# One common rank for a background step's small TensorE products, 18 instructions behind the start of the step

## The chip, the cores and the metric

The kernel runs on 1 core of one Trainium2 chip. The metric is the device time of one execution in microseconds. Five engines work side by side: TensorE (PE, with its weight loads shown as PEld), VectorE (DVE), ScalarE (ACT), GpSimd (POOL) and SyncE (SP), which issues the transfers.

## The reference

One inference step of a two-layer decoder trunk in float32, for a prompt of 1024 rows and 8 samples of 8 rows, model width 1024. Layer 0's mixer joins gated linear attention (GLA) and a depthwise convolution of 31 taps; layer 1's joins dilated windowed attention (three patterns, 4 heads each, with cached keys and values for the samples) and a chunked gMLP. After each mixer comes a convolutional FFN of inner width 2816. Cut to what matters:

```
def trunk(x, gla_s, convb_buf, kv_bufs, ffn_buf, p):
    for layer in range(DEPTH):
        h = rmsnorm(x, p['norm_pre_mix'][layer])
        if layer % 2 == 0:
            y, s_new, cb_new = even_mixer(h, ...)      # GLA | Conformer conv
        else:
            y, kv_new, v_new = odd_mixer(h, ...)       # dilated attention | gMLP
        x = x + rmsnorm(y, p['norm_post_mix'][layer])
        h = rmsnorm(x, p['norm_pre_ffn'][layer])
        f, fb = conv_ffn(h, ffn_buf[layer], ...)       # (gelu(g) * val) @ w_down
        x = x + rmsnorm(f, p['norm_post_ffn'][layer])
```

The outputs are both groups' rows and all new states and caches.

## The kernel before, in words

The rows are cut in two halves: A holds prompt rows 0 to 511 (one piece of 512 columns), B holds rows 512 to 1023 and the 64 sample rows (two pieces of 288 columns). Activations lie transposed, features on partitions.

The large products, called main products here, go through `gemm` (L374): a weight column block of 1024 x 128 is fetched (raw), split into a high and a low part (whi on ACT or POOL, wlo on DVE or POOL), and for each of up to 8 blocks of the inner dimension three products are issued per piece (whi x hi, whi x lo, wlo x hi) into a PSUM tile "g". Their tiles in the profile are "g<-...".

Everything else of a mixer (GLA, convolution, attention, gMLP, norms, loads) is written as generators. `during` (L236) makes one the background of the following main products, and `gemm` calls `pump` (L242) after each inner block; `pump` runs as many steps of the generator (each up to its next `yield`) as the amount of main work since the last call is worth. `drain` (L253) runs what is left of a generator at once, outside `pump`. The steps' own products are small; they go through `tr` (L222, transposes) and `mm` (L226) into PSUM tiles "m", of which there are four, and are copied out by ACT, DVE or both. A float32 small product shows as two MATMUL records in the profile, a main product as one. `mm` is also called by `gemm`, and `tr` by main code such as `in_odd` (L1224).

The order of work on each engine is not written by hand. Each instruction is traced with a rank, the builder's running number `cur_priority`; each traced instruction raises the number by one. The builder then orders every engine's instructions in advance: in its own model of time, an engine takes the ready instruction of the lowest rank. `high_priority(offset)` sets the number to the current one less `offset` inside its block, and sets it back to the old value on leaving, so that instructions inside the block don't advance it. The weight fetches use it already: `chunk` (L355) gives them ranks 400 ahead (`self.ahead`, L359).

The stages, in the order of the trace, with their rough places in the span:

- 0 to 358: load, input projections of layer 0 for A and B; behind them convolution and GLA of A, then the norms of A.
- 358 to 840: FFN of A, layer 0. Behind it `mix0` (L1901): convolution (L838) and GLA (L918) of B, the copy of cache rows, and the FFN state's transposes. GLA's `pairs(lv)` (L951) issues per step four copies of the query (L959, two on ACT and two on POOL, first group of a level only), four small products, and two masked copies on DVE (L983).
- 840 to 1036: output projection of B, input projection of A for layer 1; behind it the norms of B and `sgu_prepare` (L1171), the transposes of the gMLP's masked weights.
- 1036 to 1600: FFN of B, layer 0; behind it `mix1(A)` (L1926): gMLP (L1322) and attention (L1372) of A. Then output projection and norms of A.
- 1600 to 1836: start of A's second FFN and, inside it, the input projection of B for layer 1; behind it the gMLP of B and the sample scores.
- 1836 to 2097: A's second FFN goes on; behind it the sample attention (L1700) and the attention of B. 2097 to 2192: the rest of that, drained, and the output projection of B.
- 2192 to 2738: rest of A's FFN, the norms of B, B's second FFN and the end.

The lines around the change:

```
    def pump(self, units):
        ...
        while self.acc > 0:
            w = next(self.bg, None)
            ...
            self.acc -= w
```

Of the kernel before, what the change touches and what calls it, by code (L numbers as in the profile page):

```python
# [2 lines left out]

# [1 line left out]

# [123 lines left out]
class Half:  # L129
    def __init__(self, idx):  # L130
        self.i = idx
        self.t0 = 512 * idx
        self.ns = NS if idx else 0
        self.n = 512 + self.ns
        self.pieces = [(0, 288), (288, 288)] if idx else [(0, 512)]
        self.blocks = [(b * P, P) for b in range(4)] + ([(512, NS)] if idx else [])


class Kern:
    def __init__(self, ctx, tc, I, O):  # L140
        self.tc, self.nc, self.I, self.O = tc, tc.nc, I, O
        self.uid = 0
        pool = lambda name, **kw: ctx.enter_context(tc.tile_pool(name=name, **kw))
        self.cp = pool("cp", bufs=1)
        self.dp = pool("dp", bufs=1, space=DRAM)
        self.ar = [pool("arA", bufs=24), pool("arB", bufs=24)]
        self.wp = pool("wp", bufs=3)
        self.ap = pool("ap", bufs=10)
        self.fp = pool("fp", bufs=2)
        self.np_ = pool("np", bufs=1)  # L150
        self.mp = pool("mp", bufs=2)
        self.pg = pool("pg", bufs=4, space=PSUM)
        self.pm = pool("pm", bufs=4, space=PSUM)
        self.halves = [Half(0), Half(1)]
        self.rr = 0
        self.copy_act = False
        self.urgent = [0, 0]
        self.bg = None
        self.ahead = 0

        self.nw, self.hi_act, self.lo_pool = 0, 0, 0


# [57 lines left out]

    def tr(self, out, in_):  # L222
        k = in_.shape[0]
        self.nc.tensor.transpose(out, in_, self.ident[:k, :k])  # L224

    def mm(self, out, l, r, start, stop):  # L226
        self.nc.tensor.matmul(out, l, r, start=start, stop=stop)  # L227

    def rstd(self, out, in_, scale):

# [11 lines left out]
    def pump(self, units):  # L242
        if self.bg is None:
            return
        self.acc += units * self.rate
        while self.acc > 0:
            w = next(self.bg, None)
            if w is None:
                self.bg = None
                return  # L250
            self.acc -= w
# [1761 lines left out]
```

## Time and profile before

| | us |
|---|---|
| median of 3 runs | 2743.64 |
| lowest and highest | 2735.56, 2754.35 |
| the profiled execution | 2739.51 |
| its span | 2737.7 |
| TensorE busy | 2602.5 |
| VectorE busy | 1750.0 |

The span is the time from the first to the last instruction of one profiled execution. Busy times are unions over an engine's instructions. A row of a timeline has the start, the length, the engine, the line, the operation, output<-inputs, the shape and the count; in brackets the engine's idle time before it and what ended it. A row of the waits has the time in all, how often, and the longest. PEclk is TensorE's granted clock as a share of full speed (2.4 GHz; the lower level is half of it).

### The profile page before, as it was taken

The page shows a single profiled execution, that of the slowest core. Times are in us where ns is not written, and L with a number is a line of the kernel's source. Part 1 is how long each engine was busy: PE and PEld are TensorE (multiplying, and loading weights), DVE is VectorE, ACT ScalarE, POOL GpSimd, SP SyncE. Part 2 cuts the span into 40 slices and gives each one's busy share as a digit, 9 for nine tenths or more (in the row PEclk, how much of TensorE's full clock was granted, in tenths as well). Part 3 has the DMA queues.
Part 4 walks back from the last instruction along what each step waited for, and adds up shares of the span by engine and source line. Part 5 has one row for each costly group of instructions (what it writes and reads, how often), then busy time and mean ns, then how long its engine had stood idle before and what let it go on. Part 6 is the DMA issues. An engine that isn't in the chain of part 4 may idle for free.

```text
span 2737.7 us, 43989 instructions
## 1 busy us (share of the span) xinstructions
PE 2602.5 (95%) x16517; PEld 2324.9 (85%) x16517; DVE 1750.0 (64%) x3045; ACT 963.7 (35%) x2022; POOL 1039.2 (38%) x1159
## 2 busy tenths in 40 slices
PE   7989999998999999999999999889999899999998
PEld 6779887786888779999999979877878678999998
DVE  4898369999577664655557784557665358555555
ACT  4343455433454222333323342113334343322223
POOL 2321333533235443242437533553213266333333
PEclk9999999999999999999999999999999799999999
DMA  7433354454544464332324335884454152422232
GB/s 218 127 99 92 91 194 148 151 161 146 173 126 134 144 192 121 115 96 81 89 70 137 122 112 177 234 247 136 124 169 133 34 172 85 141 78 74 82 91 82
DMA packets 505004, 355.83 MB, mean 130 GB/s; under 512 B 29547, under 2 KB 461282, under 8 KB 504015
## 3 DMA queue, kind: packets, MB, share of 16 engines
q1 hardware_dynamic: 504791, 353.01, 42.8%
q8 instruction: 131, 2.15, 0.3%
q14 instruction: 82, 0.67, 0.1%
HBM read 306.43 MB, written 75.97 MB: 140 GB/s over the span
## 4 chain that ended last, share of the span: by engine, by line
PE 62%; DVE 11%; DMA 6%; POOL 4%; issue 2%; ACT 2%; SPq 1%; POOLq 0%; DVEq 0%; ACTq 0%
PE g L227 55%; PE m L227 6%; DVE cv L200 3%; DMA kc<-qr 2%; PE m L224 2%; DVE wlo L371 2%; DVE c L200 1%; POOL whi L206 1%; DVE y L197 1%; SPq L188 1%; DVE y L200 1%; DMA raw<-in_w_down 1%; POOL ss L427 1%; DVE lo L197 1%; POOL w L1691 1%
## 5 line engine op out<-in xcount | busy, mean ns | idle before, releaser
L227 PE MATMUL g<-hi,whi 128*128 128x288 f32 (+2 forms) x4440 | 1272.6, 335 | 33.9 <-ACT hi L209 9.8
L227 PE MATMUL g<-lo,whi 128*128 128x288 f32 (+2 forms) x4440 | 1260.4, 332 | 5.3 <-DVE lo L197 5.3
L227 PE MATMUL g<-hi,wlo 128*128 128x288 f32 (+1 forms) x4416 | 1248.8, 332 | 4.2 <-DVE wlo L371 2.9
L227 PEld LDWEIGHTS g<-hi,whi 128*128 128x128 f32 (+1 forms) x4440 | 773.9, 191 | 108.3 <-issue 23.5
L227 PEld LDWEIGHTS g<-lo,whi 128*128 128x128 f32 (+1 forms) x4440 | 773.5, 190 | 68.0 <-DVE lo L197 7.7
L227 PEld LDWEIGHTS g<-hi,wlo 128*128 128x128 f32 x4416 | 768.6, 191 | 65.7 <-DVE wlo L371 4.1
L371 DVE TENSOR_TENSOR wlo<-raw,whi 128x1024 fp32r<-128x1024 f32 (+2 forms) x382 | 408.0, 1068 | 440.9 <-POOL whi L206 340.8
L206 POOL TENSOR_SCALAR whi<-raw 128x1024 fp32r<-128x1024 f32 (+2 forms) x307 | 318.3, 1037 | 704.2 <-PE g L227 568.2
L371 POOL TENSOR_TENSOR wlo<-raw,whi 128x1024 fp32r<-128x1024 f32 (+2 forms) x94 | 194.7, 2073 | 405.8 <-ACT whi L209 357.5
L200 DVE SCALAR_TENSOR_TENSOR c<-u,dw,c 128x512 f32<-128x512 f32 (+3 forms) x528 | 317.4, 638 | 44.5 <-ACT c L212 42.7
L209 ACT ACTIVATE whi<-raw 128x1024 fp32r<-128x1024 f32 (+3 forms) x171 | 145.0, 849 | 382.4 <-PE g L227 256.2
L209 ACT ACTIVATE u<-g 128x224 f32<-128x224 f32 (+2 forms) x352 | 129.1, 398 | 296.6 <-PE g L227 284.1
L200 DVE SCALAR_TENSOR_TENSOR cv<-u,cvw,cv 128x512 f32<-128x512 f32 (+21 forms) x240 | 192.6, 813 | 1.9
L197 DVE TENSOR_TENSOR y<-y,g 128x288 f32<-128x288 f32 (+3 forms) x240 | 120.2, 526 | 111.8 <-PE g L227 111.5
L212 ACT ACTIVATE c<-g,dw 128x288 f32<-128x288 f32 (+1 forms) x264 | 173.1, 657 | 2.0 <-DVE lo L197 1.0
L427 POOL TENSOR_TENSOR ss<-ss,sq 128x512 f32<-128x512 f32 (+1 forms) x75 | 121.3, 1618 | 40.8 <-ACT sq L212 37.7
L209 ACT ACTIVATE hi<-c 128x512 fp32r<-128x512 f32 (+1 forms) x88 | 57.9, 658 | 199.2 <-DVE c L197 199.1
L212 ACT ACTIVATE c<-c 128x512 f32<-128x512 f32 (+1 forms) x88 | 57.9, 658 | 145.0 <-DVE c L200 137.3
L600 POOL COPY last<-u 128x2 f32<-128x2 f32 x88 | 49.2, 559 | 115.1 <-ACT u L209 102.4
L212 ACT ACTIVATE sq<-y 128x512 f32<-128x512 f32 (+3 forms) x103 | 63.2, 622 | 83.9 <-POOL ss L427 44.3
L200 DVE SCALAR_TENSOR_TENSOR y<-y,vec,rb 128x512 f32<-128x512 f32 (+1 forms) x104 | 87.6, 909 | 7.0 <-ACT rb L209 7.0
L1691 POOL TENSOR_TENSOR w<-kc,kc 128x512 f32<-128x512 f32 x48 | 65.0, 1369 | 69.9 <-DMA kc<-qr 64.4
(288 smaller groups left out, 2246.0 us busy)
## 6 DMA issues: line engine op xcount, KB each, us to landing
raw<-in_w_up SPq DMA_DIRECT2D x176, 512.0 KB
raw<-in_w_down SPq DMA_DIRECT2D x128, 256.0 KB
raw<-in_w_in_odd SPq DMA_DIRECT2D x44, 512.0 KB
raw<-in_w_in_even SPq DMA_DIRECT2D x40, 512.0 KB
out_s_kv<-in_cache_c_w SPq DMA_DIRECT2D x32, 512.0 KB
raw<-in_w_down SPq DMA_DIRECT2D x64, 192.0 KB
xl<-x SPq DMA_DIRECT2D x40, 256.0 KB
kc<-in_cache_c_w SPq DMA_DIRECT2D x80, 128.0 KB
```

The source lines that it names most:

```text
L188: self.nc.sync.dma_start(out, in_)
L197: self.nc.vector.tensor_tensor(out=out, in0=a, in1=b, op=op)
L200: self.nc.vector.scalar_tensor_tensor(out=out, in0=a, scalar=s, in1=b, op0=op0, op1=op1)
L206: self.nc.gpsimd.tensor_scalar(out=out, in0=a, scalar1=s1, scalar2=s2, op0=op0, op1=op1)
L209: self.nc.scalar.activation(out, in_, AF.Copy, scale=scale)
L212: self.nc.scalar.activation(out, in_, func, **kw)
L224: self.nc.tensor.transpose(out, in_, self.ident[:k, :k])
L227: self.nc.tensor.matmul(out, l, r, start=start, stop=stop)
L371: eng.tensor_tensor(out=wlo[:, :nk, :m], in0=raw[:, :nk, :m], in1=whi[:, :nk, :m].bitcast(F32), op=ALU.subtract)
L427: eng.tensor_tensor(out=t, in0=t, in1=sq, op=ALU.add)
L600: self.nc.gpsimd.tensor_copy(self.last2[l][:, jt, :], u[:, 512:514])
L1691: nc.gpsimd.tensor_tensor(out=pr, in0=kc.rearrange("p i c -> p (i c)"), in1=q.rearrange("p i c -> p (i c)"), op=ALU.mult)
```

## The change

`pump` notes the rank at which a step starts (`place`). While a step runs, `tr` and `mm` trace their instruction inside `high_priority` with an offset that makes its rank `place + 18`, whatever its own place in the step. Instructions of the step on other engines and its transfers keep their ranks; so do main products and drained work, as `place` is None there.

```
+        self.lag, self.place = 18, None
...
     def tr(self, out, in_):
         k = in_.shape[0]
-        self.nc.tensor.transpose(out, in_, self.ident[:k, :k])
+        with self.behind():
+            self.nc.tensor.transpose(out, in_, self.ident[:k, :k])
 
     def mm(self, out, l, r, start, stop):
-        self.nc.tensor.matmul(out, l, r, start=start, stop=stop)
+        with self.behind():
+            self.nc.tensor.matmul(out, l, r, start=start, stop=stop)
+
+    def behind(self):
+
+        if self.place is None:
+            return nullcontext()
+        return self.tc.high_priority(self.tc.cur_priority - self.place - self.lag)
...
         while self.acc > 0:
+            self.place = self.tc.cur_priority
             w = next(self.bg, None)
+            self.place = None
```

## Rows read from the trace of the kernel before

**Rows 1.** The page: span and busy time of each engine.

```profile
span 2737.7 us, 43989 instructions
...
PE 2602.5 (95%) x16517; PEld 2324.9 (85%) x16517; DVE 1750.0 (64%) x3045; ACT 963.7 (35%) x2022; POOL 1039.2 (38%) x1159
```

**Rows 2.** Busy time by stage; columns as in the first line.

```profile
core 0: us, PE busy (x) PEld busy (x) DVE busy (x) ACT busy (x) POOL busy (x), PEclk, DMA share, GB/s
...
358.00:840.00 482.00, 458.85 (x2325) 375.13 (x2323) 393.21 (x699) 214.29 (x387) 163.18 (x124) 0.96 0.47 152
...
1036.00:1600.00 564.00, 553.99 (x3921) 524.94 (x3921) 338.90 (x662) 184.61 (x445) 246.91 (x355) 0.99 0.35 104
1600.00:1836.00 236.00, 213.44 (x1429) 199.77 (x1428) 130.65 (x187) 58.52 (x124) 107.36 (x92) 0.98 0.70 203
...
2097.00:2192.00 95.00, 81.34 (x682) 64.91 (x682) 34.83 (x102) 35.69 (x88) 21.56 (x30) 0.82 0.26 78
```

**Rows 3.** TensorE's waits: us in total, times, longest us.

```profile
PE m L227 <- POOL ss L427: 9.8, 3, 3.5
PE g L227 <- ACT hi L209: 9.8, 4, 5.1
...
PE m L227 <- DVE kt L197: 8.8, 4, 2.6
...
PE g L227 <- ACT c L212: 7.0, 2, 5.2
...
PE m L227 <- POOL w L959: 5.0, 1, 5.0
```

**Rows 4.** Busy time of the instructions on tile "m", all stages (PE, PEld, DVE, ACT).

```profile
sum 2738.00, PE 367.57 PEld 293.56 DVE 178.43 ACT 97.91; mean PE 40.84 PEld 32.62 DVE 19.83 ACT 10.88
```

**Rows 5.** Timeline of TensorE, a GLA step in the first FFN.

```profile
526.78 0.39 PE L227 MATMUL g<-hi,wlo 128*128 128x512 f32 x1
...
530.86 0.39 PE L227 MATMUL g<-hi,wlo 128*128 128x512 f32 x1
...
536.99 1.65 PE L227 MATMUL m<-w,k 128*128 128x128 f32 x6 [4.97 <-POOL w L959]
```

**Rows 6.** Timeline of TensorE, main products of 288 columns.

```profile
1190.78 0.42 PE L227 MATMUL g<-lo,whi 128*128 128x288 f32 x2
...
1191.31 0.43 PE L227 MATMUL g<-hi,whi 128*128 128x288 f32 x2
```

**Rows 7.** Timeline of POOL, the copy of line 959.

```profile
525.44 11.50 POOL L959 COPY w<-q 64x256 f32<-64x256 f32 x1 [0.94 <-DVE q L197]
```

**Rows 8.** Timelines of TensorE, the gMLP of B and its weights' mask.

```profile
1735.82 0.66 PE L227 MATMUL m<-sg,kt 128*64 128x128 f32 x8 [2.30 <-DVE kt L197]
...
1754.32 0.66 PE L227 MATMUL m<-sg,kt 128*64 128x128 f32 x8 [2.38 <-DVE kt L197]
...
973.95 0.33 PE L224 MATMUL m<-ident,w 128*128 128x128 f32 x1 [1.93 <-DVE w L197]
```

**Rows 9.** Busy time and granted clock behind two waits (columns as in rows 2).

```profile
1754.00:1758.00 4.00, 3.68 (x21) 3.51 (x22) 0.95 (x2) 0.00 (x0) 1.27 (x1) 0.60 0.81 238
...
536.00:543.00 7.00, 6.01 (x17) 5.04 (x18) 7.00 (x11) 0.88 (x2) 5.08 (x5) 0.52 0.36 119
```

**Rows 10.** Timeline, a round of the attention of A.

```profile
1200.08 0.60 PE L224 MATMUL m<-ident,S 128*128 128x128 f32 x4
1200.71 0.60 ACT L209 ACTIVATE w<-m 128x512 f32<-128x512 f32 x1 [1.97 <-PE m L224]
...
1204.59 0.66 PE L227 MATMUL m<-w,v 128*64 128x128 f32 x8
```

**Rows 11.** Busy time in two parts of the first FFN (columns as in rows 2).

```profile
479.00:684.00 205.00, 191.27 (x960) 154.20 (x959) 192.70 (x350) 79.97 (x133) 79.07 (x49) 0.96 0.48 152
684.00:821.00 137.00, 137.00 (x668) 111.85 (x667) 86.18 (x156) 63.22 (x124) 40.55 (x46) 1.00 0.48 150
```

**Rows 12.** Masked copies of the GLA of B: ns min/median/max, first and last start.

```profile
L983 DVE COPY_PREDICATED AT<-lev,m x26: 211/428/817, 479.3 to 611.5; 128x256 f32<-128x256 int8 x20, 64x64 f32<-64x64 int8 x6
```

More of the change, by code (lines that the diff above doesn't have):

```diff
@@ L1 @@
 import math
-from contextlib import ExitStack
+from contextlib import ExitStack, nullcontext
 import numpy as np
```

## The prediction

> **What bounds the kernel now.** I read the page first, then the waits of TensorE, the busy time by stage, and at the longest waits the timeline. The page shows one bound: TensorE is busy 95% of the span of 2737.7 us and no other engine over 64% [rows 1]. What is not TensorE work is 2737.7 - 2602.5 = 135 us. Besides, the granted clock falls to its lower level (1.2 GHz) after some waits; a stage's figure below 1.00 shows it [rows 2]. So a change of TensorE's order can win only from these two, and only where a wait lies before a small product that a background step issues, or is caused by one.
>
> The list of TensorE's waits says how much that is [rows 3]. Small products ("m") wait for inputs of many kinds, a few us each: 9.8 us for the sum of squares, 8.8 for the gMLP's normalised rows, 5.0 for one POOL copy. The small products take 368 us of TensorE in all [rows 4], and the stages where the two longest mixers run behind an FFN (358 to 840, 1036 to 1600) lose 482 - 458.9 = 23.1 and 564 - 554.0 = 10.0 us of idle time [rows 2].
>
> **Which products the new rank moves.** The builder issues, on each engine, the ready instruction of lowest rank. A step starts at rank P. Before, its products had ranks P, P+1, and so on; the next product of the main matrix multiplication stands behind the whole step. After, all its products have P+18, and since an instruction traced inside the guard does not advance the count, the main stream resumes at P+n, with n the step's instructions on other engines. So a ready product now goes 18 - n main products later, and one with n above 18 goes as before. This bites only where the product was ready when the main stream stood within 18 ranks of P. Where the step's inputs come late, the main stream is long past P+18 and both ranks are lower than anything outstanding: nothing changes. Setting the program's ranks beside its order on TensorE (an order, no times) gives 1,784 products issued by pumped steps: 290 go out with the main stream 0 to 17 ranks past P, the others with it further past, or still behind P and blocked. Of the 290, 123 belong to the GLA and the convolution of the second half behind the first FFN (358 to 840), 122 to the attention of the first half (1036 to 1600), and 20 to the gMLP of the second half and what is around it. In the sample attention (1836 to 2097) the steps are 250 to 800 ranks behind: 0 of them move. The drained tail behind it, 2097 to 2192, which has 81.3 us of work in 95 us at 0.82 of the clock [rows 2], is traced outside steps and keeps its ranks.
>
> **What it gives, step by step.** One lag first. In the first FFN the 19th main product of a run starts 4.08 us after the first (526.78, 530.86 [rows 5]), 0.227 us for each, and a GLA level step has n = 6 (four copies, two masked copies), so its products go 12 main products or 2.7 us later. With 288 columns four products take 0.53 us (1190.78 to 1191.31 [rows 6]), 0.133 each.
>
> 1. The 4.97 us wait at 536.99 [rows 5]. Its step is one of the 123. The product waits for a POOL copy that took 11.50 us [rows 7], which the builder's own durations did not foresee, or it would have put the product later. 2.7 us more of main products fit in front of it: the wait falls to 2.3 us. Gain 2.7 us; bounds 0 (the main stream is itself blocked there) and 5.0.
> 2. The gMLP's four waits of 8.8 us [rows 3]. n = 4 gives 14 main products; before, those at 1735.82 and 1754.32 (2.30 and 2.38 us [rows 8]) already went 3 behind the step, so 11 x 0.133 = 1.5 us each. For the other two the main stream was 42 and 20 ranks past P, so they don't move. Gain 3.0 us; bounds 0 and 4.7.
> 3. The wait of 1.93 us at 973.95 for the gMLP weights' mask [rows 8]: its step has n = 3, so 15 main products, of which 12 were already in front; 3 main products more, 3 x 0.227 = 0.7 us; bounds 0 and 1.9.
> 4. The waits for the sum of squares, [rows 3], for the gate input and for the combine stand far behind P, or before it, or outside a step: 0.
>
> Sum of idle time: 6.4 us. The clock after these waits: 0.52 over the 7 us from 536 and 0.60 over the 4 us from 1754 [rows 9]. Back at full speed these would take 7 x 0.52 and 4 x 0.60, so 3.4 and 1.6 us less. As both waits shrink and don't vanish I take half, 2.5 us; bounds 0 and 5.0. Together 8.9 us, bounds 0 and 17.
>
> **What it costs.** No instruction is added. No wait is added to TensorE either: a later place can only find its input more finished. What waits longer is the step's next instruction: ACT's or DVE's copy out of PSUM, by 1.1 to 4 us (8 to 18 main products), and what stands behind it in that engine's order. The attention of the first half shows what hides it: a transpose at 1200.08, its copy at 1200.71, the product from the copy only at 1204.59 [rows 10]. The copy takes 0.60 us, so over 3 us lie unused between it and the product; both go back by up to 18 x 0.133 = 2.4 us, the product by as much as the transpose, and the distance stays. In the first FFN the DVE has less room (rival D). At the end of a window a step's results come at most 18 main products late, 4.1 us at 0.227; there the main stream goes on with work that needs them only behind its own copies and splits. I take 2 us for all windows, bounds 0 and 35 (rival D). No DMA issue changes its rank. The weight fills keep "400 ranks ahead", and since about 1,800 products are no longer counted in the 21,400 ranks, 400 ranks reach some 8% further back; the weight buffers (two raw, three split) bound that before the rank does: 0. PSUM's four "m" buffers are taken when a product issues, so they are held no longer than before: 0.
>
> Net 8.9 - 2 = 7 us off. The profiled execution took 2739.5 us around its span of 2737.7, 4 us under the median of the three runs, 2743.6. 2739.5 - 7 = 2732.5; carried over to the median, 2743.6 - 7 = 2737 us. That is 0.3%, and about 1% is what a measurement of this kernel can tell from no change.
>
> How much could be won at most depends on what counts as idle. The trace's gaps say 135 us. The Trainium skill, in "Perfetto Trace Analysis", section "Identifying the Most-Contended Engine", says that busy time of matrix products is a bad measure of the distance to the limit, and that the weight loads' busy share should be used; by that measure 2737.7 - 2324.9 = 413 us would be open, and a better order could be worth three times as much as I allow. This trace does not bear it out: from 684 to 821 TensorE's products fill 137.00 of 137 us while the weight loads fill 111.9 [rows 11]: a fifth of the loads' time is open and no product waits. I keep 135.
>
> **The rivals.**
> A (the forecast, 0.48): a few waits shrink, 2737 us; its own range 2722 to 2752.
> B (0.22): the lag does nothing that can be measured, since 1,494 of 1,784 products don't move and the waits at 536.99 and 1754 re-form elsewhere, as they come from durations that the builder has wrong: 2744 us. For it: the largest wait hangs on a single copy of 11.50 us. Against: two more waits move by a fixed count.
> C (0.17): moving 245 products in the two FFN stages also dissolves waits of the main stream there, such as 5.2 us on an ACT output and 9.8 us on a split [rows 3], by letting main products run ahead. 358 to 840 and 1600 to 1836 hold 23.1 + 22.6 us of idle time, and (1 - 0.96) x 482 + (1 - 0.98) x 236 = 24 us of lost clock [rows 2], 70 us; half of it gives 2709 us. Against: the main waits that I can follow come from DVE's and ACT's own queues, not from products.
> D (0.13, the other side): DVE pays. From 479 to 684 DVE is busy 192.7 of 205 us [rows 11] with the convolution, and the GLA's masked copies sit in its queue: 26 between 479.3 and 611.5 [rows 12], two for each of 13 steps. If each step's copy now stands waiting 2.7 us in DVE's order with convolution and split work behind it, DVE loses 13 x 2.7 = 35 us where it has 12 to spare, and the main stream's sums and splits come late: up to 2779 us. It decides from the point where the builder places the copy by its own clock and TensorE on the chip is later than that. Against: the builder fills DVE by readiness, so it moves the copy behind convolution work.
>
> **How the numbers follow.** Chances: A 0.48, B 0.22, C 0.17, D 0.13. Time 2737. The range leaves out half of D and the better end of C: 2708 to 2766. Faster by over 1% (under 2716): C with a little of A, 0.18. Slower by over 1% (over 2771): D and a little of a general reshuffle, 0.13. Within 1%: 0.69.
>
> **What would show it.** Right: the wait of a small product on the POOL copy at 536.99 falls from 5.0 to about 2.3 us, the gMLP waits from 8.8 to about 5.8; TensorE's busy time stays within a few us of 2602; the sample attention and the tail around 2097 to 2192 look as before. A is wrong if the waits of small products stay and the span falls all the same, or if waits of the main stream ("g") for DVE's sums and ACT's splits grow in the first FFN (that is D). If small products in the sample attention change their place, my reading of which products move is wrong.

## The result, and the profile after

The change makes the kernel slower. Six executions of it lie between 2754.5 and 2768.6 us, median 2760.6; six of the kernel before between 2735.6 and 2754.4, median 2743.2. The ratio is 1.0065, with a 95% interval of 1.0046 to 1.0083: some 17 us, where 7 us off were forecast. That is less than the 1% that the prediction took as the least that a measurement of this kernel can tell, but the interval excludes no change, and each of the six is above the slowest of the six before (by 0.1 us at the least). The profiled execution took 2762.3 us.

The page of the kernel after, span and busy time, beside [rows 1]:

```profile
span 2760.5 us, 43972 instructions
...
PE 2630.3 (95%) x16517; PEld 2337.7 (85%) x16517; DVE 1751.2 (63%) x3045; ACT 962.5 (35%) x2022; POOL 1019.4 (37%) x1159
```

This is the first thing to see: the span grew by 22.8 us, and TensorE's busy time by 27.8. Its idle time (span less busy) fell, from 135.2 to 130.2 us. So it is not more waiting that made the kernel slower; TensorE was occupied for longer with the same 16,517 matrix records. (Part of the 27.8 us is the clock of these two executions, as told below.)

Two stages of the kernel after, beside [rows 2]:

```profile
358.00:840.00 482.00, 460.72 (x2284) 372.90 (x2283) 391.60 (x695) 212.52 (x378) 151.84 (x121) 0.96 0.48 151
...
1036.00:1600.00 564.00, 556.69 (x3907) 523.73 (x3906) 327.40 (x647) 179.07 (x437) 237.26 (x352) 1.00 0.35 104
```

In the stage of the attention of A (1036 to 1600) TensorE is busier than before and issues 14 records fewer. It idles less (7.3 us against 10.0), the clock is full, and still the work takes longer: 6.7 us more between the same two main products of the attention. (The order of the main products is the same in both kernels, so a stretch can be compared between the same two of them. Here and below they are named by their time in the kernel before: this stretch is 1175 to 1400.)

The waits of TensorE after, beside [rows 3] (us in total, times, longest):

```profile
PE m L231 <- DVE kt L199: 14.5, 4, 7.2
PE g L231 <- ACT hi L211: 12.8, 5, 4.9
...
PE m L231 <- POOL ss L439: 7.4, 3, 3.5
...
PE g L231 <- ACT c L214: 5.6, 2, 5.2
```

The 5.0 us behind the POOL copy are gone (0.4 us are left on that line); the gMLP's waits grew from 8.8 to 14.5.

Where the time went shows in the busy time of the small products, kept apart by shape. First the window 1036 to 1600 of the kernel before (shape of the weights, output, count, then busy us and mean ns of one):

```profile
L227 PE MATMUL m<-k,q 64*128 64x128 f32 x72 | 12.6, 402 | 0.0
L227 PE MATMUL m<-w,v 128*64 128x128 f32 x120 | 10.1, 286 | 0.0
L224 PE MATMUL m<-ident,S 128*128 128x128 f32 x60 | 9.0, 272 | 0.0
```

and the same view of the kernel after:

```profile
L231 PE MATMUL m<-k,q 64*128 64x128 f32 x72 | 15.4, 406 | 0.0
L231 PE MATMUL m<-w,v 128*64 128x128 f32 x120 | 13.1, 289 | 0.0
L227 PE MATMUL m<-ident,S 128*128 128x128 f32 x60 | 10.3, 273 | 0.0
```

The counts are the same and each instruction is as long as it was to 1%, but the products on keys and on values (k,q and w,v) cover 2.8 and 3.0 us more: they overlap each other less. (The transposes cover 1.3 us more as well; one of the experiments shows that theirs costs no time.) The timeline says why. A round of the attention of A before, on TensorE:

```profile
1194.25 0.42 PE L227 MATMUL g<-hi,wlo 128*128 128x288 f32 x2
1194.60 0.66 PE L227 MATMUL m<-w,v 128*64 128x128 f32 x8
1195.19 0.53 PE L227 MATMUL g<-hi,whi 128*128 128x288 f32 x2
```

and after:

```profile
1198.88 0.42 PE L231 MATMUL g<-hi,wlo 128*128 128x288 f32 x2
1199.23 0.43 PE L231 MATMUL m<-w,v 128*64 128x128 f32 x2
1199.59 0.40 PE L231 MATMUL g<-hi,whi 128*128 128x288 f32 x1
1199.92 0.65 PE L231 MATMUL m<-w,v 128*64 128x128 f32 x6
1200.50 0.40 PE L231 MATMUL g<-hi,whi 128*128 128x288 f32 x1
```

Before, the eight records (four float32 products, for two heads and two blocks) stand in one run. After, one main product stands behind the first product. All products of a step share the rank P+18 now, and one main product has just that rank. The builder takes the ready instruction of the lowest rank and has to break the tie: the main product comes out between the first of the step's products and the rest.

What this costs can be read off, from start to start. One run: 1194.60 to 1195.19, 0.59 us. In two: 0.36 (1199.23 to 1199.59), the main product in between 0.33 (to 1199.92), the rest 0.58 (to 1200.50). A main product among its own takes 0.13 [rows 6]. So 1.27 us against 0.59 + 0.13 = 0.72: 0.55 us for one main product in the wrong place. Three products take as long as four, one as long as two would.

Counted in the two traces, stretches of small products between main ones rose from 363 to 401, in the gMLP and attention of A (1036 to 1440) from 55 to 77. Between their first and last main product the two profiles differ by 22.6 us. I split that at each main product into idle time, time lost at the lower clock, and what a run of small products takes over the main products' pace. Idle time gave 5.5 us back, the clock took 10.2, the 38 further runs took 17.1, main products among themselves 0.7. The 10.2 us of clock are not the change: the mean granted clock of the six executions after was 0.969 to 0.974, and that of the 82 executions of the kernel before that ran beside the experiments 0.966 to 0.976, with half of them at 0.970 or above. The execution shown here for before (0.975) is at the upper end of its own. What remains beside the clock is 12 us; the medians say 17, and single executions of one kernel lie up to 19 us apart (2735.6 to 2754.4).

### The profile page after: what moved, and what is told of

The parts are those of the page before. It is cut to its first block, busy times and chain, and to the rows that moved or that the text cites. A ratio compares the mean times of both kernels' runs of the same rounds, so it can differ in the third digit from the quotient of the medians.

```text
span 2760.5 us, 43972 instructions
## 1 busy us (share of the span) xinstructions
PE 2630.3 (95%) x16517; PEld 2337.7 (85%) x16517; DVE 1751.2 (63%) x3045; ACT 962.5 (35%) x2022; POOL 1019.4 (37%) x1159
## 4 chain that ended last, share of the span: by engine, by line
PE 62%; DVE 11%; DMA 6%; POOL 4%; issue 3%; ACT 2%; SPq 1%; POOLq 0%; DVEq 0%; ACTq 0%
PE g L231 55%; PE m L231 6%; DVE cv L202 3%; DMA kc<-qr 2%; DVE wlo L383 2%; PE m L227 2%; DVE c L202 1%; POOL whi L208 1%; DMA raw<-in_w_up 1%; SPq L190 1%; DVE y L199 1%; POOL w L1703 1%; DVE y L202 1%; POOL ss L439 1%; DVE lo L199 1%
## 5 line engine op out<-in xcount | busy, mean ns | idle before, releaser
L231 PE MATMUL g<-hi,whi 128*128 128x288 f32 (+2 forms) x4440 | 1276.2, 335 | 35.4 <-ACT hi L211 12.8
L383 POOL TENSOR_TENSOR wlo<-raw,whi 128x1024 fp32r<-128x1024 f32 (+2 forms) x94 | 200.7, 2136 | 409.2 <-ACT whi L211 323.3
L202 DVE SCALAR_TENSOR_TENSOR cv<-u,cvw,cv 128x512 f32<-128x512 f32 (+21 forms) x240 | 200.7, 847 | 1.8
## 6 DMA issues: line engine op xcount, KB each, us to landing
raw<-in_w_down SPq DMA_DIRECT2D x64, 192.0 KB
```

Source lines behind the costliest of these rows:

```text
L202: self.nc.vector.scalar_tensor_tensor(out=out, in0=a, scalar=s, in1=b, op0=op0, op1=op1)
L383: eng.tensor_tensor(out=wlo[:, :nk, :m], in0=raw[:, :nk, :m], in1=whi[:, :nk, :m].bitcast(F32), op=ALU.subtract)
```

## The experiments

The theory after the result: main products that fall between a step's half-array products (64 rows or 64 columns of weights) cost 0.5 to 0.7 us each. Its rival: the later place itself costs, as copies and what hangs on them come late. A third: one common rank reorders the small products among themselves. "Run" in the expectations below means a stretch of small products between two main products; the counts there are of the order that the builder gives TensorE (364 before, 402 after; the traces have one less). All times are medians, beside executions of the kernel before on the same chip (2742 to 2745 us). The differences in us are worked out from the ratio, which is not just the quotient of the two medians.

**The lag alone: 0 and 4 ranks.**

```
-        self.lag, self.place = 18, None
+        self.lag, self.place = 0, None        # second kernel: 4
```

> The common rank stays, the lag is 0: all products of a step get the step's first rank. Split theory (a main product of equal rank goes between a step's first product and its others, and each further run of small products costs some 0.5 us): 15 runs of small products more than before, 378 instead of 363, 12 of them in the attention of the first half, where products use half the array; 5 to 7 us slower than before, about 2749 us. Lateness theory (products that come 18 ranks later keep copies and the clock waiting): nothing is late, so no difference, 2743 us.

> The lag is 4 instead of 18. Split theory: ties are as frequent as with 18, 411 runs of small products, 48 more than before; 12 to 18 us slower, about 2758 us. Lateness theory: a lag of 4 leaves at most 4 main products, under 1 us, so under a quarter of the 17 us remains: about 2747 us.

Lag 0: 2752.9 us, ratio 1.0033 (1.0018 to 1.0049), 9 us slower. Lag 4: 2760.9 us, 1.0060 (1.0038 to 1.0081), 16 us slower. With no lag at all half of the loss is there, and a lag of 4 costs as much as one of 18. In the trace of lag 0 the attention of A (1175 to 1400) takes 6.7 us longer, with 12 runs more. So the loss doesn't follow how late the products come.

**The lag in one place, and everywhere else.**

```
-        if self.place is None:
+        if self.place is None or self.lag is None:
             return nullcontext()
...
         def close_a():
             self.drain()
+            self.lag = None                   # the other kernel: 18
...
+        self.lag = 18                         # the other kernel: None
         self.during(mix1(A), 63, 50)
```

> The change (lag 18, ties) only while the attention of the first half is in the background. Split theory: 22 runs more, nearly all of products on half the array: 6 to 9 us slower than before, about 2751 us. Lateness theory: in this stage the trace after shows neither more idle time nor a lower clock than before, so 0 to 2 us: about 2744 us.

> The change in all step loops but the one behind the second FFN (gMLP and attention of A): 380 runs between main products against 364 before and 402 in the change. The change costs 17 us, the lag in that one loop alone 7 us. If the parts add up: 9 to 11 us, 2751 to 2755 us. If the loss in the attention of A is what makes the rest (its late results shift what follows): 2742 to 2747 us.

In the gMLP and attention of A alone: 2753.0 us, 1.0027 (1.0011 to 1.0043), 7.4 us. Everywhere else: 2751.8 us, 1.0039 (1.0016 to 1.0062), 10.7 us. They add up to 18 us, and the change costs some 17. No single place makes the loss.

**The same lag with the tie taken away.** First by doubling: main products on even ranks, steps on odd ones.

```
     def mm(self, out, l, r, start, stop):
+        if self.place is None:
+            self.tc.cur_priority += self.tc.cur_priority % 2
...
-        return self.tc.high_priority(self.tc.cur_priority - self.place - self.lag)
+        return self.tc.high_priority(self.tc.cur_priority - (self.place + self.lag | 1))   # lag 31
```

> Main products get even ranks and the steps' products odd ones, 31 behind, which is again 12 to 14 main products behind a step with 4 to 6 other instructions; no main product ties with them. Split theory: 360 runs of small products, 3 fewer than before; the 14 us of splits go, 2741 to 2749 us, and less than 2743 if the shorter waits that were forecast come without them. Lateness theory: the same lag, so the same loss, about 2760 us.

2766.7 us, 1.0081 (1.0061 to 1.0102): the theory's forecast failed, although the trace shows the attention of A back at its old time (1.2 us less than before, 1175 to 1400). Doubling changes every other rank too, so I tried its two side effects:

```
-        self.ahead = 400
+        self.ahead = 780
```

> The run with doubled main ranks (2767 us) again, with the weight fills 780 instead of 400 ahead, since a main product now takes up to two ranks and 400 reached only half as far back. If that halved reach made its loss: 2742 to 2750 us, as the other run without ties. If doubled ranks cost for another reason: 2760 to 2768 us.

2764.3 us, 1.0076 (1.0054 to 1.0098): the shorter reach of the weight fetches was not it. Then the doubled ranks alone, with the reach of 780 and `behind` returning `nullcontext()` always:

> Main products on even ranks, the weight fills 780 ahead, and the step products at their own ranks, so no lag and no common rank: 369 runs against 364 before. If the doubled ranks themselves (the order against the other engines' work) made the 20 us of the two runs without ties: 2755 to 2768 us. If the later place made them: 2742 to 2748 us.

2766.1 us, 1.0082 (1.0058 to 1.0105). The doubling costs the 22 us by itself, without any lag or common rank, so neither of the two runs speaks about the tie. Which of the orders that it changes is the dear one stays open; in the trace 14.8 us more lie in the stretch of the sample attention (1836 to 2097), which holds 33 more small products than before, and 6.6 less in the tail behind it, from which they come.

The clean way leaves every rank as it is, and has a main product pass over a rank that a step has taken:

```
     def mm(self, out, l, r, start, stop):
+        while self.place is None and self.tc.cur_priority in self.taken:
+            self.tc.cur_priority += 1
...
+        self.taken.add(self.place + self.lag)
         return self.tc.high_priority(self.tc.cur_priority - self.place - self.lag)
```

> The change as it is (lag 18, one common rank), but a main product never takes the rank of a step's products: its number is raised by one where it would. Unlike the run with doubled ranks nothing else moves: the weight fills stay 400 ahead. In the builder's order the small products then come in 367 runs between main products, against 364 before and 402 in the change. Split theory (0.5 to 0.7 us for each run more of half-array products): 3 runs more, about 2 us; with other small shifts 2742 to 2750 us, where before is 2744. Lateness theory (products 18 ranks late hold up the copies and what follows): as the change, 2757 to 2764 us.

> As the run with lag 0, but without a main product of the same rank between a step's products: 366 runs against 378 with lag 0 and 364 before; attention of A 56 as before. Split theory: 12 runs fewer than with lag 0, so 7 to 8 us of its 9 us go: 2743 to 2748 us. If it is the common rank itself (the order among the small products of neighbouring steps, above all in the sample attention), the loss stays: about 2752 us.

Lag 18: 2744.9 us, 1.0008 (0.9991 to 1.0024). Lag 0: 2747.5 us, 1.0008 (0.9991 to 1.0026). Both kernels with a tie were slower by 0.65% and 0.33%; without it neither can be told from before. With the lag of 18 the two intervals, with the tie and without, lie apart. With the lag of 0 they overlap, and the traces decide: from 1175 to 1400 the kernel with the tie takes 6.7 us more than before, the one without it 0.0 (with the lag of 18: 6.7 more with the tie, 1.5 less without). So the lag of 18 has no cost and no gain that these times can tell. The small products of lag 18 without ties, window 1036 to 1600:

```profile
L233 PE MATMUL m<-k,q 64*128 64x128 f32 x72 | 12.6, 402 | 0.0
L233 PE MATMUL m<-w,v 128*64 128x128 f32 x120 | 10.1, 286 | 0.0
```

To the tenth these are the numbers of before. The rounds come later on TensorE, but whole.

The third theory holds for a part. Split as above, the small products of the two kernels without ties still take 7.4 us (lag 18) and 7.5 us (lag 0) more over the main pace than before, with only 3 and 2 runs more. The common rank changes the order of small products within their runs too, and skipping leaves that as it is. So of the 17.1 us in the trace after, about 10 go with the tie. TensorE's idle time fell by some 10 to 13 us in these two traces and their lower clock took 12 to 15; since idle time fell with no lag as well, it is not a gain of the lag.

**More of it, by kind of product.** In the gMLP and attention of A alone, with the skip above, each matrix product of a step gets its own rank, two behind the one before it. In the counterpart the transposes get them, and in a third kernel pairs of matrix products do.

```
+        at = self.place + self.lag + 2 * self.j     # pairs: self.j = self.c // 2
+        self.j += spread                            # 1 for products, 0 for transposes, or the reverse
+        self.taken.add(at)
+        return self.tc.high_priority(self.tc.cur_priority - at)
```

> Lag 18 in the step loop behind the second FFN alone (gMLP and attention of A). The matrix products of one step get ranks 18, 20, 22 and so on behind the step, the transposes one common rank; so main products fall between the half-array products: 105 runs there against 56 before and 78 with ties, 411 in all against 364. Split theory: 47 to 49 runs more at 0.5 to 0.7 us, 24 to 34 us: 2768 to 2778 us. Lateness theory: at most 2755 us, as the run with lag 18 in attention A alone (2753) and little more.

> The counterpart: the transposes of one step (full 128 x 128 products) get ranks 18, 20, 22 behind the step, its matrix products one common rank that no main product shares. 84 runs there against 56 before, 390 in all against 364. If only runs of half-array products cost: 23 of the 28 runs more are of transposes and free, the rest some 3 us: 2744 to 2750 us. If any return from main products to small ones costs 0.6 us: 26 to 28 runs, 2759 to 2762 us.

> As the run with spread matrix products in the attention of A (2770 us, 105 runs there), but the two products of the two heads that follow each other keep one rank, so that main products fall only between pairs: 75 runs there against 56 before, 19 more. If each run more costs 0.5 to 0.6 us, however it is cut: 10 to 12 us, 2751 to 2756 us. If the price is the pair's lost overlap on the halves of the array, and whole pairs can be parted for nothing: 2742 to 2747 us.

Products spread: 2770.2 us, 1.0095 (1.0067 to 1.0123). Transposes spread: 2742.4 us, 1.0001 (0.9981 to 1.0021). Pairs spread: 2748.1 us, 1.0024 (1.0010 to 1.0039). Products apart cost 26 us for 47 runs more; transposes apart cost nothing that can be told for 26 runs more. The pairs fell between the two answers that I had written down: 6.6 us for 19 runs. The timelines show the two parts of the price. Products one by one:

```profile
1193.04 0.42 PE L233 MATMUL g<-hi,wlo 128*128 128x288 f32 x2
1193.39 0.43 PE L233 MATMUL m<-w,v 128*64 128x128 f32 x2
1193.75 0.40 PE L233 MATMUL g<-hi,whi 128*128 128x288 f32 x1
1194.08 0.43 PE L233 MATMUL m<-w,v 128*64 128x128 f32 x2
```

Pairs:

```profile
1195.11 0.44 PE L233 MATMUL m<-w,v 128*64 128x128 f32 x4
1195.47 0.40 PE L233 MATMUL g<-hi,whi 128*128 128x288 f32 x1
1195.81 0.44 PE L233 MATMUL m<-w,v 128*64 128x128 f32 x4
1196.17 0.41 PE L233 MATMUL g<-hi,whi 128*128 128x288 f32 x1
```

One product (x2) holds TensorE for 0.36 us until the next main product, 1193.39 to 1193.75. A pair (x4) holds it for the same 0.36, 1195.11 to 1195.47: the two heads' products, which have 64 columns of weights each and go to the two halves of the partitions, run side by side. And the main product between takes 0.33 or 0.34 us instead of 0.13. So parting two pairs costs 0.36 + 0.34 + 0.36 - 0.59 - 0.13 = 0.34 us, all of it spent where TensorE goes to the main product and back. Four products apart take 4 x 0.36 + 3 x 0.33 = 2.43 us instead of 0.59 + 3 x 0.13 = 0.98, or 0.48 for each cut: here the pairs are lost as well. The tie of the change is of this second kind, as it cuts behind the first product of a pair (0.55 us). Transposes one by one:

```profile
1208.79 0.30 PE L233 MATMUL g<-lo,whi 128*128 128x288 f32 x1
1208.93 0.27 PE L227 MATMUL m<-ident,S 128*128 128x128 f32 x1
1208.95 0.38 PE L233 MATMUL g<-lo,whi 128*128 128x288 f32 x1
1209.17 0.27 PE L227 MATMUL m<-ident,S 128*128 128x128 f32 x1
```

These use the whole array, as main products do. A main product follows 0.02 us behind the start of a transpose, the next transpose 0.22 us later: 0.24 us for the two. Among its own kind the main product takes 0.13, and in a run of four, as from 1200.08 to the main product at 1200.43 before [rows 10], a transpose takes 0.09 (it shows as one record, not two as the other small products do). That is 0.02 us for parting them. The main product meant, in the trace before:

```profile
1200.43 0.51 PE L227 MATMUL g<-hi,whi 128*128 128x288 f32 x2
```

The Trainium skill states half of this price as a rule: "TensorEngine Tiling (Array Packing)", section "Key Properties", says that TensorE drains when the tiling mode changes, not when merely the tile does, and that tiles can work side by side. These traces agree and put a number on it: 0.33 us for a main product between two half-array products, 0.13 among its own kind, and no surcharge between main products and 128 x 128 transposes.

**Later still, and gathered.** With the skip, lags of 100 and 250, and steps rounded up to a common rank:

```
-        self.lag, self.place, self.taken = 18, None, set()
+        self.lag, self.place, self.taken = 100, None, set()      # 250
...
-            self.place = self.tc.cur_priority                    # gathered: lag 0 and
+            self.place = -(-self.tc.cur_priority // 128) * 128
```

> A step's products at one common rank 100 behind its start, which no main product shares. 348 runs between main products against 364 before, 240 of them with matrix products against 241. If only the split runs cost and lateness is free: 2738 to 2747 us, no difference that can be told from before. If a later place costs by itself and 18 ranks are too few to show it: over 2752 us.

> The same with 250 ranks, more than most steps need to have their inputs finished: 327 runs, 230 with matrix products (11 fewer than before, at 0.6 us some 7 us), and fewer waits of small products. Lateness free: 2730 to 2743 us, which would beat both kernels. Lateness costs: steps of a chain (scores, softmax, transposes, products) each come up to 250 ranks late and the background spills out of its stages, over 2755 us.

> Ranks of steps are rounded up to the next multiple of 128, so the products of all steps that begin within 128 ranks share one place; no main product shares it. 333 runs, 239 with matrix products. Split theory: 2736 to 2747 us. A cost of the common order of several steps' products: over 2752 us.

Lag 100: 2767.1 us, 1.0086 (1.0066 to 1.0107). Lag 250: 2840.8 us, 1.0361 (1.0342 to 1.0381). So the rival isn't wrong in itself: a later place does cost, but far beyond 18 ranks. The page of lag 250:

```profile
span 2842.5 us, 44000 instructions
...
PE 2653.3 (93%) x16517; PEld 2355.5 (83%) x16517; DVE 1737.4 (61%) x3045; ACT 967.3 (34%) x2024; POOL 995.5 (35%) x1159
```

Here TensorE does stand idle, 189 us instead of 135, and the clock falls with it (0.954). That is how lateness looks at its plainest, and the kernel after doesn't look so. At lag 100 it doesn't show as idle time (135.3 us, as before): there the trace has 9.2 us more over the main pace, with 16 runs fewer, and 17.9 us more at the lower clock. How much of its loss is lateness stays open.

Gathered steps: 2785.6 us, 1.0153 (1.0134 to 1.0173), with fewer runs than before. My split theory as it stood (so much for each run) had no room for that; TensorE's timeline has:

```profile
1275.35 0.43 PE L233 MATMUL m<-w,v 128*64 128x128 f32 x2
1275.71 0.48 PE L233 MATMUL m<-k,q 64*128 64x128 f32 x2
1276.12 0.43 PE L233 MATMUL m<-w,v 128*64 128x128 f32 x2
1276.49 0.49 PE L233 MATMUL m<-k,q 64*128 64x128 f32 x2
1276.90 0.43 PE L233 MATMUL m<-w,v 128*64 128x128 f32 x2
```

Two steps with one rank come out alternately, a product with 64 columns and one with 64 rows of weights, 0.36 to 0.41 us each where four of one kind take 0.59 together. So a neighbour of another shape costs within a run too; in this trace the runs, 31 fewer, took 42 us more over the main pace than before. The price is one for what stands next to what, not for a run. Whether the change of shape itself or the parted pairs make it, these rows can't tell apart.

No kernel of these beats the one before. The nearest, transposes spread (1.0001) and the two skips (1.0008), can't be told from it.

## Why the prediction was wrong

The time lies inside the range (2708 to 2766) and within 1%, but 17 us on the slower side of before, where the forecast had 7 on the faster. By its own steps:

- **Which products move.** Partly right. The attention of A and the first FFN are where the new rank bites, as said. The sample attention and the tail were to look as before, and do not: even with lag 0 and no ties 92 runs lie there (1836 to 2192) instead of 87, since a common rank also reorders small products among themselves. In the seven traces with a common rank 0 to 100 behind the step there and ranks not doubled, ties or not, the stretch from 1836 to 2097 takes 5.7 to 10.1 us more than before, 2.3 to 3.0 of them for small products over the main pace and 1.7 to 5.1 for the clock; in the four with a lag in the gMLP and attention of A alone it takes between 0.6 less and 0.5 more. The whole times without ties (1.0008) don't show it, so other stretches gave it back, or it lies in the noise; which, stays open.
- **Step 1, the wait at 536.99.** The gain came (4.97 to 0.4 us, forecast 2.3), but not because products were put in front of it: the copy that took 11.50 us took at most 1.63 us in the kernel after. The last section says more. No run shows that the lag as such would have taken the wait down to 2.3.
- **Step 2, the gMLP.** Wrong: 14.5 us instead of 5.8. One wait of 7.2 us makes half of it; without ties the sum was 9.3. What put DVE's rows so late there is not isolated.
- **Step 3, the mask.** Wrong but small: 1.93 us before, 1.99 us after, at 984.64.
- **The sum of idle time.** 6.4 us off were forecast, 5.0 came (130.2 against 135.2), but that is luck: the waits named in steps 1 to 3 grew by 1.2 us together, the rest came from others, and the four traces with the lag in the attention of A alone have 126.1 to 132.3. The 2.5 us from the clock can't be seen: they would be 0.001 of the mean clock, and single executions differ by up to 0.010.
- **What it costs.** This step failed: "No instruction is added. No wait is added to TensorE either: a later place can only find its input more finished." It took a product's price to be the same wherever it stands. The common rank changes what stands next to what, and that is a price of TensorE's own, 17.1 us in the trace: about 10 of them go with the tie between a step's products and one main product, some 7 are of the small products' order among themselves and stay without it. The sign that was named for it, TensorE's busy time within a few us of 2602, failed (2630.3). By the ratios 7 us arise in the gMLP and attention of A and 11 elsewhere, and all but some 2 us are gone once the tie is taken away: in those traces TensorE also stands idle for less time, so its remaining price doesn't reach the span in full. The sum read 8.9 - 2; lag 18 without ties measures these two terms together, with what the small products' order costs, and there they come to 2 us slower (2.5 faster to 7 slower) instead of 7 faster.
- **The rivals.** D fell: DVE is busy 192.0 of the 205 us from 479 to 684, as before [rows 11]. So did C: the main stream's waits did not dissolve, those for ACT's split rose from 9.8 to 12.8 us. B's outcome (nothing to be measured) is what the change would have been without the tie. The mechanism that decided was in none of them, though rows of the kernel before held it: the eight records of [rows 10] fill 0.66 us at a mean of 286 ns each, so they cover each other, and that cover can be lost.

## What to carry to other kernels

In this kernel an order in which small products of part of the array alternate with full ones, or with another shape, costs TensorE 0.34 to 0.55 us for each cut by a full one, and no list of waits shows it: look for the same count and the same mean length, and more busy time. When ranks are given out by hand, ask what else has the same rank, and keep products that use different parts of the array next to each other. And before a "later" is costed at nothing, count the changes of neighbours on the engine, not only the inputs.

## What the runs showed of the hardware beside that

The copy of 11.50 us on POOL [rows 7] seems to be a matter of its neighbours on DVE. POOL's timeline of the kernel before, behind that copy:

```profile
536.91 2.36 POOL L371 TENSOR_TENSOR wlo<-raw,whi 128x1024 fp32r<-128x1024 f32 x1
```

DVE's at the same time:

```profile
535.01 0.27 DVE L200 SCALAR_TENSOR_TENSOR cv<-us,cvw,cv 128x64 f32<-128x64 f32 x1
...
535.87 0.74 DVE L200 SCALAR_TENSOR_TENSOR cv<-u,cvw,cv 128x512 f32<-128x512 f32 x1
536.53 2.81 DVE L200 SCALAR_TENSOR_TENSOR cv<-us,cvw,cv 128x64 f32<-128x64 f32 x1
539.27 0.21 DVE L582 COPY fst<-m 128x64 f32<-128x64 f32 x1
```

While the copy lasts, DVE works without a gap, mostly on its convolution. When POOL goes on with its split, a DVE instruction takes 2.81 us, ten times the 0.27 us of its equals just before, and ends at 539.34, as the split does at 539.27. The times fit two engines that hold each other up; no run changes one of them alone, so it is argued and not shown. All POOL copies of this line, before and after (ns, least, median and most):

```profile
L959 POOL COPY w<-q x20: 388/540/11498, 180.8 to 577.3; 64x256 f32<-64x256 f32 x20
```

```profile
L971 POOL COPY w<-q x20: 390/504/1632, 179.8 to 581.5; 64x256 f32<-64x256 f32 x20
```

The most was 1.6 to 2.3 us in the eight kernels with gathered steps or a lag of 4, 18, 31 or 250 in the first FFN, and 11.5 us in all eight without a lag there and in the one with a lag of 100: it goes with the order of the work, and is not chance. The Trainium skill, "SBUF — State Buffer", section "SBUF: two separate sides", has a rule that fits: DVE, with two inputs in SBUF, and GpSimd share a pair of ports that the first holds for its whole instruction while the other waits. The 2.81 us agree with it; that a copy waits past many DVE instructions, as the 11.50 us suggest, is more than it says.
